# SwiGLU over 8192 rows: a first load in four interleaved transfers, an early gate on eight zeros, and five stores on GpSimd

## The chip, the cores and the metric

The kernel runs on one core of one Trainium2 chip. The metric is the device time of the whole program in microseconds (us), lower is better.

## The reference

```python
def reference(x):                      # x: 8192 x 8192, float32
    a, b = np.split(x, 2, axis=-1)     # two halves of 4096 columns
    silu_b = b / (1 + np.exp(-b))
    return a * silu_b                  # 8192 x 4096, float32
```

Every input element is read once (268.44 MB) and every output element written once (134.22 MB).

## The kernel before, in words

The 8192 rows are cut into 33 tiles in order of rows. Tile 0 and tile 32 have one row of x for each of the 128 partitions; the 31 tiles between have two. One row of x is 32 KB, so a full tile is loaded with 64 KB for each partition (8.39 MB) and stored with 32 KB for each (4.19 MB); tile 0 and tile 32 are half of that.

Three buffers in SBUF, `slot0` to `slot2`, take the tiles in turn: tile i lies in slot i modulo 3. For each tile there are four steps, and each belongs to one engine:

- `load` (line 51) is a DMA issued on SyncE (SP). Tile i+3 goes into the slot of tile i, so its load waits on SP until the store of tile i has landed.
- the gate (line 62) is SiLU on ScalarE (ACT), in place on the b half.
- the product (line 64) is a multiplication on VectorE (DVE), written over the front of the slot.
- `store` (line 77) is a DMA that waits for the product. It is issued from ACT's queue for tiles 0 to 29, and from SP's queue for tiles 30 to 32. Two of the earlier ones go to GpSimd (POOL) in place of ACT: the odd tiles from 16 to 19, that is 17 and 19.

The order of the instructions is the written one (`manual_schedule`): three loads first, then for each tile its gate, product, store, and the load three tiles ahead. Tiles 0 and 32 are gated and multiplied in two halves of 2048 columns, tiles 1 and 31 row by row. `follows_from_others` drops waits that are implied by others; `newest` remembers the last instruction on each engine for it. A DMA with 128 partitions is spread over the core's 16 DMA engines, with a packet for each contiguous row of a partition, and 16 small packets that signal its completion.

Of the kernel before, what the change touches and what calls it, by code (L numbers as in the profile page):

```python
# [1 line left out]

# [4 lines left out]

_SILU = mybir.ActivationFunctionType.Silu


@with_exitstack
def kernel(
    ctx: ExitStack,
    tc: tile.TileContext,
    x: bass.AP,
    out: bass.AP,
):

    nc = tc.nc  # L20
    N, M = x.shape
    half = M // 2
    P = nc.NUM_PARTITIONS
    BUFS = 3

    rows = [1] + [2] * (N // P // 2 - 1) + [1]
    first = [sum(rows[:i]) * P for i in range(len(rows))]
    last = len(rows) - 1

    pool = ctx.enter_context(tc.tile_pool(name="sbuf", bufs=1))  # L30
    ctx.enter_context(tc.manual_schedule())
    slots = [pool.tile([P, 2 * M], x.dtype, name=f"slot{s}") for s in range(BUFS)]
    loads, gates, prods, stores = ([[] for _ in rows] for _ in range(4))
    newest = {}

    def in_dram(t, i, width):

        return bass.AP(t.tensor, first[i] * width, [[rows[i] * width, P], [1, rows[i] * width]])

    def follows_from_others(inst, i, current, earlier):  # L40


        targets = [t for kind in current for t in kind[i]]
        targets += [t for kind in earlier for j in range(i % BUFS, i, BUFS) for t in kind[j]]
        for t in targets:
            if t is not newest.get(inst.ins.engine):
                tc.declare_no_dep(inst.ins, t.ins, reason="ordered by the other waits")
        newest[inst.ins.engine] = inst

    def load(i):  # L50
        inst = nc.sync.dma_start(  # L51
            out=slots[i % BUFS][:, : rows[i] * M], in_=in_dram(x, i, M)
        )
        follows_from_others(inst, i, [], [loads, gates, prods])
        loads[i].append(inst)

    def swiglu(i, k0, k1, c0=0, cw=half):
        view = slots[i % BUFS].rearrange("p (k s c) -> p k s c", k=2, s=2)
        a = view[:, k0:k1, 0, c0 : c0 + cw]
        b = view[:, k0:k1, 1, c0 : c0 + cw]  # L60
        o = slots[i % BUFS][:, : 2 * half].rearrange("p (k c) -> p k c", k=2)
        gate = nc.scalar.activation(out=b, in_=b, func=_SILU)  # L62
        follows_from_others(gate, i, [], [loads, gates, prods, stores])
        prod = nc.vector.tensor_mul(out=o[:, k0:k1, c0 : c0 + cw], in0=a, in1=b)  # L64
        follows_from_others(prod, i, [loads], [loads, gates, prods, stores])
        gates[i].append(gate)
        prods[i].append(prod)

    def by_halves(i):
        for c0 in range(0, half, half // 2):  # L70
            swiglu(i, 0, 1, c0, half // 2)

    def store(i):
        eng = nc.scalar if i < last - 2 else nc.sync
        if i % 2 and last // 2 <= i < last // 2 + 4:
            eng = nc.gpsimd
        inst = eng.dma_start(  # L77
            out=in_dram(out, i, half), in_=slots[i % BUFS][:, : rows[i] * half]
        )
        follows_from_others(inst, i, [loads, gates], [loads, gates, prods, stores])  # L80
        stores[i].append(inst)

    for i in range(BUFS):
        load(i)
    for i in range(last):
        if i == 0:
            by_halves(i)
        elif i in (1, last - 1):
            swiglu(i, 0, 1)
            swiglu(i, 1, 2)  # L90
        else:
            swiglu(i, 0, rows[i])
        store(i)
        if i + BUFS <= last:
            load(i + BUFS)
    by_halves(last)
    store(last)


# [1 line left out]
_INS = ['x']  # L101
_OUTS = [((8192, 4096), 'float32')]


# [23 lines left out]
```

## Time and profile before

| | us |
|---|---|
| median of three runs | 935.03 (934.96, 935.03, 940.76) |
| the profiled execution, its own time | 934.94 |
| span of its profile | 933.2 |
| DVE busy | 278.7 (30%) |
| ACT busy | 226.8 (24%) |
| POOL busy | 1.4 |
| moved by DMA | 402.67 MB, mean 432 GB/s |

The time of a run has 1.74 us beside the span of the profile. In the views, a line such as `L51 SPq DMA_DIRECT2D slot<-in_x_dram` is a DMA issue of line 51 on SP's queue; "to landing" is the time from the issue until the transfer's completion is signalled. The table of windows gives for each stretch of the span the busy time of the engines with the number of instructions, then the DMA share (1.00 is all 16 DMA engines busy) and GB/s. It counts a packet where it starts, so in very short windows it can be read as a count of packets: 32 KB in 0.25 us is 131 GB/s.

### The profile page before, as it was taken

Reading aid. Unit: us, or ns where it says so; the run is one execution under the profiler, and the core shown is the slowest. Engines: PE = TensorE matmul, PEld = TensorE weight load, DVE = VectorE, ACT = ScalarE, POOL = GpSimd, SP = SyncE. Lnnn points to the kernel's source line nnn. Section 1 sums busy time; section 2 is a strip of 40 time slices with the busy share of each in tenths; the row PEclk is TensorE's granted clock in tenths of the full one; section 3 lists DMA queues with packets and bytes.
Section 4 is the critical chain, followed back from the end, with each engine's and each line's share of the span. In section 5 each row is a group of like instructions: output and inputs, shape, how many; then the busy total and the mean of one; then the engine's idle time right before and its main releaser. Section 6 shows DMA issues by size and latency. Waiting matters only on the chain.

```text
span 933.2 us, 220 instructions
## 1 busy us (share of the span) xinstructions
DVE 278.7 (30%) x37; ACT 226.8 (24%) x38; POOL 1.4 (0%) x6
## 2 busy tenths in 40 slices
DVE  1312333123331233312333113332133321333242
ACT  2331133311333203332033320233202332023330
POOL 0000000000000000000000000000000000000000
DMA  9999999999999999999999999999999999999998
GB/s 405 405 449 431 423 451 444 409 444 433 444 427 434 442 410 448 428 433 442 434 421 441 445 417 444 428 454 427 420 457 405 449 427 428 448 445 409 427 444 388
DMA packets 9505, 402.67 MB, mean 432 GB/s; under 512 B 1056, under 2 KB 1056, under 8 KB 1056
## 3 DMA queue, kind: packets, MB, share of 16 engines
q1 hardware_dynamic: 5184, 278.92, 69.1%
q10 hardware_dynamic: 4032, 115.35, 28.6%
q0 software_dynamic: 288, 8.39, 2.1%
q14 instruction: 1, 0.01, 0.0%
HBM read 268.44 MB, written 134.22 MB: 431 GB/s over the span
## 4 chain that ended last, share of the span: by engine, by line
DMA 72%; DVE 11%; ACT 8%; issue 6%; another core or an unknown queue 1%; DVEq 0%; POOL 0%; SPq 0%; ACTq 0%; POOLq 0%
DMA slot<-in_x_dram 40%; DMA out_dram<-slot 32%; DVE slot L64 11%; ACT slot L62 8%; DVEq L123 0%; POOL out_dram L77 0%; SPq L51 0%; ACTq L77 0%; DVEq L64 0%; POOLq L123 0%
## 5 line engine op out<-in xcount | busy, mean ns | idle before, releaser
L64 DVE TENSOR_TENSOR slot<-slot 128x8192 f32<-128x8192 f32 (+2 forms) x37 | 278.7, 7539 | 636.7 <-ACT slot L62 636.5
L62 ACT ACTIVATE slot<-slot 128x8192 f32<-128x8192 f32 (+2 forms) x37 | 225.6, 6107 | 684.3 <-DMA slot<-in_x_dram 684.3
L77 POOL DMA_DIRECT2D out_dram<-slot x2 | 1.2, 600 | 568.9 <-DVE slot L64 568.9
L62 ACT ACT_TABLE_LOAD x1 | 1.3, 1283 | 0.7 <-PEq L112 0.7
L112 POOL MEMSET const-bfloat16-1.0<- 128x1 bf16 x1 | 0.1, 102 | 0.0
L112 POOL MEMSET const-float32-0.0<- 128x1 f32 x1 | 0.1, 99 | 0.2 <-issue 0.2
L112 POOL MEMSET const-float32-1.0<- 128x1 f32 x1 | 0.1, 99 | 0.0
L112 POOL MEMSET const-uint8-127<- 128x1 uint8 x1 | 0.1, 99 | 0.0
## 6 DMA issues: line engine op xcount, KB each, us to landing
out_dram<-slot ACTq DMA_DIRECT2D x27, 4096.0 KB, 33.5
slot<-in_x_dram SPq DMA_DIRECT2D x2, 4096.0 KB, 13.6
out_dram<-slot POOLq DMA_DIRECT2D x2, 4096.0 KB, 34.4
out_dram<-slot SPq DMA_DIRECT2D x2, 4096.0 KB, 20.4
out_dram<-slot ACTq DMA_DIRECT2D x1, 2048.0 KB, 28.1
out_dram<-slot SPq DMA_DIRECT2D x1, 2048.0 KB, 16.8
slot<-in_x_dram SPq DMA_DIRECT2D x31, 37.7
```

The costliest lines, as they stand in the source:

```text
L62: gate = nc.scalar.activation(out=b, in_=b, func=_SILU)
L64: prod = nc.vector.tensor_mul(out=o[:, k0:k1, c0 : c0 + cw], in0=a, in1=b)
L77: inst = eng.dma_start(out=in_dram(out, i, half), in_=slots[i % BUFS][:, : rows[i] * half])
L112: nc = _bacc.Bacc("TRN2", target_bir_lowering=False, num_devices=1)
```

## The change

The first load is no longer one transfer of 128 partitions but four, all on SP and one behind the other: partitions 0, 8, 16, ... (16 of them), then 4, 12, 20, ... (16), then 2, 6, 10, ... (32), then all the odd ones (64). Ahead of them, VectorE sets eight columns of `slot2` to zero and ScalarE runs SiLU on them; the load of tile 2, which writes the same slot, waits for that. And the odd tiles stored through GpSimd are those from 16 to 25: 17, 19, 21, 23 and 25, five in place of two.

```diff
+    def load_in_parts(i):
+
+        width = rows[i] * M
+        for p0, step in ((0, 8), (4, 8), (2, 4), (1, 2)):
+            inst = nc.sync.dma_start(
+                out=slots[i % BUFS][p0::step, :width],
+                in_=bass.AP(
+                    x.tensor, first[i] * M + p0 * width, [[step * width, P // step], [1, width]]
+                ),
+            )
+            newest[inst.ins.engine] = inst
+            loads[i].append(inst)
+
...
-        if i % 2 and last // 2 <= i < last // 2 + 4:
+        if i % 2 and last // 2 <= i < last // 2 + 10:
             eng = nc.gpsimd
...
-    for i in range(BUFS):
+
+    corner = slots[2][:, :8]
+    nc.vector.memset(corner, 0.0)
+    nc.scalar.activation(out=corner, in_=corner, func=_SILU)
+    load_in_parts(0)
+    for i in range(1, BUFS):
         load(i)
```

## The prediction

> **What bounds the kernel now.** I read the page first. No engine is busy for a third of the span, while the DMA row is full in every slice:
>
> ```profile
> DVE 278.7 (30%) x37; ACT 226.8 (24%) x38; POOL 1.4 (0%) x6
> DMA  9999999999999999999999999999999999999998
> q1 hardware_dynamic: 5184, 278.92, 69.1%
> q10 hardware_dynamic: 4032, 115.35, 28.6%
> q0 software_dynamic: 288, 8.39, 2.1%
> ```
>
> The shares of the three queues (SP's q1, ACT's q10, POOL's q0) add to 99.8% of what 16 DMA engines could do in the span. The chain that ended last names waits, but in a kernel whose transfers never pause they are a queue's length, not a cost. The windows say the same by stage; the columns are the stretch, its length, DVE, ACT and POOL busy, PE clock, DMA share, GB/s:
>
> ```profile
> 1.50:1.75 0.25, 0.00 (x0) 0.25 (x1) 0.00 (x0) 1.00 0.47 131
> 1.75:2.00 0.25, 0.00 (x0) 0.25 (x1) 0.00 (x0) 1.00 6.55 1704
> 2.00:2.25 0.25, 0.00 (x0) 0.01 (x1) 0.00 (x0) 1.00 0.45 131
> 2.25:2.50 0.25, 0.00 (x0) 0.00 (x0) 0.00 (x0) 1.00 0.40 131
> 2.50:3.50 1.00, 0.00 (x0) 0.00 (x0) 0.00 (x0) 1.00 0.00 0
> 3.50:3.75 0.25, 0.00 (x0) 0.00 (x0) 0.00 (x0) 1.00 1.21 524
> 3.75:4.00 0.25, 0.00 (x0) 0.00 (x0) 0.00 (x0) 1.00 2.42 1049
> 4.00:4.25 0.25, 0.00 (x0) 0.00 (x0) 0.00 (x0) 1.00 1.21 524
> ...
> 424.60:511.60 87.00, 26.09 (x4) 21.09 (x3) 0.00 (x0) 1.00 1.00 434
> 511.60:598.60 87.00, 26.08 (x4) 21.09 (x3) 1.20 (x2) 1.00 1.00 431
> 598.60:685.60 87.00, 25.92 (x3) 21.09 (x3) 0.00 (x0) 1.00 1.01 438
> ```
>
> Read as counts, 131 GB/s being one 32 KB packet, one DMA engine starts its first packet in 1.50 to 1.75, thirteen in the next quarter, one each in the two after: 16. The second packets start from 3.50 to 4.25 (4, 8, 4), so a first packet occupies its engine some 1.9 us. A later one takes 1.21 us (in 3.50 to 3.75 four packets fill a share of 1.21: 1.21 x 0.25 x 16 / 4), and 16 x 32768 B / 1.21 us is 433 GB/s, the rate of every later window. So the span is 1.9 us until the engines run, 0.7 us more for their first packet, then solid transfer to the end, and a last landing. Three things alone can move the time: the start, the rate, or a gap in the transfers. At 434 GB/s the 402.67 MB need 927.8 us, so no reordering can bring 1%, which is 9.35 us and about what a measurement of this kernel can tell from no change.
>
> **The change part by part.** *The split load.* It replaces one DMA issue by four on SP, with the same 128 packets of 32 KB and 48 more completion packets (three transfers of 16). SP's rows:
>
> ```profile
> 0.74 1.32 SPq L51 DMA_DIRECT2D slot<-in_x_dram  x3
> L51 SPq DMA_DIRECT2D slot<-in_x_dram x33: 327/328/425, 0.7 to 893.0; - x33
> DMA to landing us min/median/max: 12.2/37.7/59.2
> ```
>
> Three issues take 1.32 us from 0.74, so the fourth part is out by about 2.3, and tiles 1 and 2 are issued some 1.0 us (3 x 0.33) later, at about 2.5 and 2.8. Each DMA engine then has one packet from part 1 until about 3.75, one from part 2, two from part 3 and four from part 4: about eight packets to 12.5, before it needs tile 1. The delay of 1.0 us is covered by some 10 us of queued work; without that cover it would cost 1.0.
>
> What can be gained is the start. A transfer with one row per DMA engine has an eighth of the rows to prepare. The end is set by the last DMA engine, so at best its start moves from the 2.25 to 2.50 window to the 1.50 to 1.75 one (0.75 us), and the whole start cannot come before the issue itself has ended, at 1.1 (0.9 us from 2.0, where most have started). At worst nothing is gained. The nearest row is the spread itself: the stragglers start 0.25 to 0.5 us behind the thirteen. I take 0.3 us, and keep 0 and 0.9.
>
> What can be lost is the rate of the narrow parts; the trace has no transfer of fewer than 128 partitions. Lower bound 0: transfers that follow one another on SP leave no gap, for a window of 87 us with six transfers runs at 434, the packet rate itself. Upper bound: tile 0 took 12.2 us from issue to landing (the minimum above), its 4.19 MB at 433 GB/s are 9.7, so a transfer by itself has 2.5 us of fixed time; if each of three more parts paid that in full, 7.5 us. In between, if each new part paid a first packet's surplus, 0.7 us, it is 3 x 0.7 = 2.1. I take 0, since back-to-back transfers are the nearest row, and keep 7.5. The 48 completion packets cost nothing that a window shows: a boundary every 14.5 us leaves the rate at the packet rate.
>
> [...]
>
> *The early gate.* It adds one memset of 128x8 on DVE and one SiLU of 128x8 on ACT. The table load that stands before ACT's first gate is there already, and early:
>
> ```profile
> 0.73 1.28 ACT L62 ACT_TABLE_LOAD   x1 [0.73 <-PEq L112]
> 12.95 3.71 ACT L62 ACTIVATE slot<-slot 128x2048 f32<-128x2048 f32 x2 [10.94 <-DMA slot<-in_x_dram]
> ```
>
> It ends at 2.01, and ACT then idles 10.94 us. POOL's memsets of 128x1 take 0.1 us and a 2048-column gate 1.9, so the added pair costs between 0.1 and 2 us, nearer the former, inside that idle time: nothing, and nothing gained, since no table load stood on the path. But it adds a wait: tile 2's load stands on SP until the tiny gate is done, about 2.3 to 2.5, at most 4.0. Behind it on SP only tile 3's load is queued, which waits for the store of tile 0 until 47 anyway. Two tiles (12.6 MB, 29 us) are ahead of tile 2's packets. Cost 0; without that cover up to 1.2 us.
>
> *Three more stores on POOL* (21, 23, 25). They leave ACT's queue, where a store waits for DVE and holds the next gate; that gate waits for its load far longer (684.3 us in 33 waits), so nothing is gained. What POOL's queue costs is read from tiles 17 and 19:
>
> ```profile
> L77 POOL DMA_DIRECT2D out_dram<-slot x2: 533/600/667, 511.9 to 570.0; - x2
> out_dram<-slot ACTq DMA_DIRECT2D x27, 4096.0 KB, 33.5
> out_dram<-slot POOLq DMA_DIRECT2D x2, 4096.0 KB, 34.4
> ```
>
> The issue takes 0.60 us against 0.34, the landing comes 0.9 us later, and SP's load of tile i+3 waits for it. Three of these are 2.7 us of lateness, under a DMA that is full in those windows (431 and then 438 GB/s around the two, 434 in the mean). After them, the chain has stores of about 31.2 and loads of 40 us where it had 33.5 and 37.6: the shares shift, their sum stays at 71. On POOL's own queue nothing else stands. At the tail the shift matters most: tile 30's store is issued at 893.4 and lands 24.4 us later, at about 918, and tile 31's store is issued at about 911, so 7 us of overlap cover it. Two POOL stores moved the shares by 2.3 us; three more in proportion move 3.5, under 7. Cost 0; bounds from a gain of 0 (a full DMA gives none) to 2.7.
>
> [...]
>
> **Sum.** Against the profiled execution: 934.94 - 0.3 + 0 + 0 + 0 = 934.6 us (span 932.9 and the same 1.74 around it); 935.03, the median of the runs, lies 0.09 above that execution, so the two are the same.
>
> **The rivals.**
>
> *The parts do not start earlier* (the split does nothing of what it could): 934.9. For it: the first packet's 1.9 us is not the number of rows but a latency. Against: 16 starts spread over three quarters of a microsecond in the order of a preparation.
>
> *Each part pays a first packet's surplus:* 934.6 + 2.1 = 936.7. For it: first packets do take 0.7 us more. Against: back-to-back transfers show none.
>
> *The narrow parts run at a fraction of the rate*, on the other side, slower: if 16 or 32 partitions do not keep 16 DMA engines at 1.21 us a packet, nothing behind on the same queue can fill in, because tile 1 is behind them. Price 7.5 us, so 942.1; it decides as soon as the load of tile 0 lands later than now (12.95). Only at half rate for the whole load (9.7 us, 944.3) does it reach 1%.
>
> *The POOL stores open a gap:* 2.7 us, so 937.3, from the point at which the transfers still queued after a landing are less than 0.9 us of work. Against: the windows stay at 1.00 around the two that exist.
>
> **How the numbers follow.** Forecast 0.45; no earlier start 0.17; first-packet surplus 0.20; narrow parts slow 0.10; gap by POOL 0.08. The time is the forecast's, 934.6, with its own range 934.0 to 935.2 (the start's bounds and the distance of the runs shown). The low end of the whole range is the earliest start (0.9 us) with the same distance, 933.8. The high end takes in the surplus and the gap together, 934.6 + 2.1 + 2.7 = 939.4; only the slow parts, and a median among runs like 940.76, lie above. By cases, over 1% slower needs the half-rate load or more: 0.04. Over 1% faster has no mechanism: 0.01. Within 1%: 0.95.
>
> **What would show it.** In the profile after: first packets in a narrower band before 2.25; tile 0 landing at or before 12.95 (right) or after 14 (the narrow parts are slow, and 934.6 is wrong by what it is late); q0 at 720 packets with 431 to 438 GB/s in the windows of tiles 17 to 25; tile 2's issue before 4. A DMA share under 0.99 in any window between 20 and 890 would make the POOL part wrong.

## The result and the profile after

The changed kernel takes 936.95 us (median of 22 runs, 936.51 to 937.29) against 935.02 us of the kernel before (median of 22): 1.9 us more. The ratio is 1.0016, with a 95% interval of 1.001 to 1.0022. The move is small (0.2%), but it is resolved, and it goes the other way from the forecast of 934.6: it lies outside the forecast's own range (934.0 to 935.2) and inside the whole one (933.8 to 939.4). The ratios here and below are not quotients of the two medians; where an interval takes in 1.0, a difference of medians is unresolved.

The profiled execution took 936.83 us with a span of 934.8, so 1.6 of the 1.9 us lie inside the span; the other 0.3 is in what lies around it (2.03 against 1.74; over the 22 runs it was 1.73 to 2.19, with a median of 2.1). The three kernels below with one part of the change each have 1.72 to 1.84 there, so no single part shows this 0.3, and it stays open. From the page of the changed kernel, its engines, DMA row and queues:

```profile
DVE 278.7 (30%) x38; ACT 227.0 (24%) x39; POOL 3.0 (0%) x9
DMA  9999999999999999999999999999999999999999
q1 hardware_dynamic: 5232, 278.92, 69.2%
q10 hardware_dynamic: 3600, 102.76, 25.5%
q0 software_dynamic: 720, 20.97, 5.2%
```

The transfers still fill the span: 69.2 + 25.5 + 5.2 = 99.9%. SP's q1 has the 48 completion packets more (5184 to 5232), and q0 has gone from 288 to 720. The same windows at the start, of the changed kernel (DMA share and GB/s last; 524 GB/s in 1.00 us is 16 packets):

```profile
1.50:2.00 0.50, 0.00 (x0) 0.50 (x1) 0.00 (x0) 1.00 0.00 0
2.00:2.50 0.50, 0.00 (x0) 0.23 (x2) 0.00 (x0) 1.00 3.94 918
2.50:3.00 0.50, 0.00 (x0) 0.00 (x0) 0.00 (x0) 1.00 0.49 131
4.00:5.00 1.00, 0.00 (x0) 0.00 (x0) 0.00 (x0) 1.00 2.42 524
6.25:7.50 1.25, 0.00 (x0) 0.00 (x0) 0.00 (x0) 1.00 1.37 419
8.25:9.00 0.75, 0.00 (x0) 0.00 (x0) 0.00 (x0) 1.00 1.62 699
```

Each of the last three rows is one packet on each of the 16 DMA engines (GB/s times length is 524 KB), and the share times the length is what one packet took. The second packet, which is part 2 of the load (partitions 4, 12, ...), took 2.42 us; the third 1.37 x 1.25 = 1.71; from the fourth on 1.62 x 0.75 = 1.21, as every packet did before. And nothing starts before 2.0, where before fourteen engines had started by then. The second and third rows of packets in the kernel before:

```profile
3.50:4.25 0.75, 0.00 (x0) 0.00 (x0) 0.00 (x0) 1.00 1.61 699
4.75:5.50 0.75, 0.00 (x0) 0.00 (x0) 0.00 (x0) 1.00 1.62 699
```

Both are 1.21 us. The timeline of the changed kernel shows where the delay ends up (start, length, what):

```profile
0.74 2.52 SPq L61 DMA_DIRECT2D slot<-in_x_dram  x4
2.03 0.21 ACT L99 ACTIVATE slot<-slot 128x8 f32<-128x8 f32 x1
15.54 3.71 ACT L75 ACTIVATE slot<-slot 128x2048 f32<-128x2048 f32 x2 [13.30 <-DMA slot<-in_x_dram]
37.18 7.12 ACT L75 ACTIVATE slot<-slot 128x4096 f32<-128x4096 f32 x2 [17.93 <-DMA slot<-in_x_dram]
```

Tile 0's gate starts at 15.54 (12.95 before), 2.6 us late; tile 1's at 37.18 (35.47), 1.7 late; and the first gate of tile 31, near the end, at 900.03 (898.41), 1.6 late. So the loss is made in the first 15 us, 0.9 of it is won back by tile 1, and what is left is carried to the end nearly unchanged: with transfers that never pause, nothing behind tile 1 absorbed it.

### The profile page after: what moved, and what is told of

Read it like the earlier page. It is cut to its first block, busy times and chain, and to the rows that moved or that the text cites. A ratio compares the mean times of both kernels' runs of the same rounds, so it can differ in the third digit from the quotient of the medians.

```text
span 934.8 us, 232 instructions
## 1 busy us (share of the span) xinstructions
DVE 278.7 (30%) x38; ACT 227.0 (24%) x39; POOL 3.0 (0%) x9
## 3 DMA queue, kind: packets, MB, share of 16 engines
q1 hardware_dynamic: 5232, 278.92, 69.2%
q10 hardware_dynamic: 3600, 102.76, 25.5%
## 4 chain that ended last, share of the span: by engine, by line
DMA 72%; DVE 11%; ACT 8%; issue 6%; another core or an unknown queue 1%; SPq 0%; DVEq 0%; POOL 0%; ACTq 0%; POOLq 0%
DMA slot<-in_x_dram 39%; DMA out_dram<-slot 32%; DVE slot L77 11%; ACT slot L75 8%; SPq L61 0%; DVEq L141 0%; POOL out_dram L90 0%; ACTq L90 0%; DVEq L77 0%; POOLq L141 0%
```

## The experiments

Two theories stood against each other first. *The split:* its parts run slow by the partitions that they take, as part 2 did with 2.42 us a packet, and it carries the 1.9 us alone. *Stores, or a surplus for each transfer:* the loss comes from the POOL stores, the added wait, or a fixed price of each issue. All kernels are the one before with one edit.

**One part of the change at a time.**

```diff
# split_only
-    for i in range(BUFS):
+    load_in_parts(0)
+    for i in range(1, BUFS):
         load(i)
# gate_only
+    corner = slots[2][:, :8]
+    nc.vector.memset(corner, 0.0)
+    nc.scalar.activation(out=corner, in_=corner, func=_SILU)
# stores_only
-        if i % 2 and last // 2 <= i < last // 2 + 4:
+        if i % 2 and last // 2 <= i < last // 2 + 10:
```

> The kernel before with the split load alone (16, 16, 32, 64 partitions interleaved); no early gate, two stores on GpSimd. [...] Theory stores: the split is worth at most the later start, 0.4 us, and tile 0 lands late without the end moving.

> The kernel before with the early gate alone (eight zeros in slot2, SiLU on them, tile 2's load waits for it). Every theory but one: within 0.2 us of the kernel before. If the wait of tile 2's load on SP matters, 0.3 to 1.2 us slower.

> The kernel before with five stores on GpSimd in place of two, nothing else. [...] Theory stores: three more landings 0.9 us later each, or a slower transfer rate while they run, give 1 to 2.7 us more.

Measured, beside a kernel before at 935.09 (33 runs): the split alone 936.86 (ratio 1.0018, 1.0009 to 1.0026), the gate alone 935.16 (1.0, 0.9991 to 1.0009), the stores alone 935.38 (1.0, 0.9992 to 1.0009). The split carries the change; neither of the other two can be told from nothing (the stores are 0.3 us over by the medians). The windows of stores_only, from the first to past the last POOL store, agree:

```profile
511.00:598.00 87.00, 26.04 (x4) 21.09 (x3) 1.20 (x2) 1.00 1.00 435
598.00:685.00 87.00, 26.07 (x4) 21.09 (x3) 0.53 (x1) 1.00 1.00 434
685.00:772.00 87.00, 26.08 (x4) 21.09 (x3) 1.06 (x2) 1.00 1.00 434
```

The timeline of split_only also shows what the early gate is good for:

```profile
15.46 1.28 ACT L77 ACT_TABLE_LOAD   x1 [15.46 <-DMA slot<-in_x_dram]
```

With four transfers to wait for, the table load stands behind the wait, at 15.46 and no longer at 0.73 (with the two transfers of halves_interleaved below it is at 13.19); the early gate in the changed kernel puts it back to 0.73. It is worth 1.28 us on ACT, at a place where ACT has time: tile 0's gate starts at 16.75 there and at 15.54 in the changed kernel, tile 1's at 37.13 and 37.18. The medians of the two are 0.1 us apart; of the spans, split_only's is 0.2 longer (935.1 against 934.9), which the 0.3 around the changed kernel's span hides.

**The same split without the narrowest parts.** The first load goes in three interleaved transfers, of 32, 32 and 64 partitions.

```diff
-        for p0, step in ((0, 8), (4, 8), (2, 4), (1, 2)):
+        for p0, step in ((0, 4), (2, 4), (1, 2)):
```

> [...] Theory that any strided or narrow transfer pays a surplus of its own: 1.2 to 2 us, nearly as much as the split in four.

Measured: 935.62, ratio 1.0002 (0.9993 to 1.0011). Three strided transfers, one of them still of 32 partitions at the head, cost some 0.5 us by the medians, which the interval does not separate from none; the other 1.2 us of split_only belong to the two transfers of 16. At tile 0 the two kernels are further apart: its parts have all landed at 13.21 here and at 15.46 in split_only, where the stall at the end of this section is missing and makes up for some of it. The window of split_32_32_64 from 4 to 12 us:

```profile
4.00:12.00 8.00, 0.00 (x0) 0.00 (x0) 0.00 (x0) 1.00 1.03 442
```

These are 108 packets (442 x 8 us / 32.8 KB) of 1.03 x 8 x 16 / 108 = 1.22 us, so the two parts with a step of 4 ran at full rate. Why the third packets of the changed kernel, also with a step of 4, took 1.71 us no run settles; they start while other engines are still on part 2.

**Sets of partitions.** The next four split the first load in other ways; only the list of parts differs.

```diff
# eighths: 16 partitions each
+    parts = (0, 8), (4, 8), (1, 8), (5, 8), (2, 8), (6, 8), (3, 8), (7, 8)   # start, step
# halves_interleaved
+    parts = (0, 2), (1, 2)
# halves_contiguous
+    partitions 0:64, 64:128
# quarters_contiguous
+    partitions 0:32, 32:64, 64:96, 96:128
```

> The kernel before with the first load in eight transfers of 16 partitions (steps of 8, starting at 0, 4, 1, 5, 2, 6, 3, 7). [...] Theory fixed surplus per transfer (0.5 to 0.7 us each): 4 to 5.6 us. Theory later start alone: 0.4 us.

> The kernel before with the first load in two transfers, the even and the odd partitions. [...] Theory strides: a strided transfer of partitions is slower in itself, 1 us or more.

> The kernel before with the first load in two transfers, partitions 0 to 63 and 64 to 127, without a stride. [...] Theory strides or narrow transfers: 0 to 0.5 us more. It also shows whether the longer issue on SP (0.59 us where the whole load took 0.43) comes from the stride.

> The kernel before with the first load in four contiguous transfers of 32 partitions. [...] Theory fixed surplus per transfer: twice the cost of two halves.

| kernel (before: 935.26) | us | ratio, 95% interval |
|---|---|---|
| eighths | 943.97 | 1.0095 (1.008 to 1.011) |
| halves_interleaved | 935.55 | 1.0002 (0.9992 to 1.0012) |
| halves_contiguous | 944.74 | 1.0103 (1.0088 to 1.0118) |
| quarters_contiguous | 944.64 | 1.0101 (1.0086 to 1.0116) |

The two kernels with two transfers of 64 partitions differ by 9.2 us through nothing but which 64 partitions (and so which 64 rows of x) each transfer takes. A window of each, first halves_contiguous:

```profile
4.75:5.00 0.25, 0.00 (x0) 0.00 (x0) 0.00 (x0) 1.00 5.12 1049
slot<-in_x_dram SPq DMA_DIRECT2D x2, 2048.0 KB, 17.5
```

then halves_interleaved:

```profile
4.00:4.25 0.25, 0.00 (x0) 0.00 (x0) 0.00 (x0) 1.00 2.43 1049
slot<-in_x_dram SPq DMA_DIRECT2D x2, 2048.0 KB, 9.7
```

Both windows have eight packets (1049 / 131). They took 5.12 x 0.25 x 16 / 8 = 2.56 us each in the one and 1.21 in the other; the median time from issue to landing is 17.5 against 9.7. The eighths, from 4 to 12 us:

```profile
4.00:12.00 8.00, 0.00 (x0) 0.00 (x0) 0.00 (x0) 1.00 1.11 242
```

That is 59 packets of 2.4 us; the same window of quarters_contiguous (1.07, 221 GB/s) has 54 of 2.54. Two contiguous halves cost as much as four quarters (944.74 and 944.64 us), so it is not a price of each transfer; and it is not the stride, since the strided halves run at full rate (1.21 us a packet). Nor is it the longer issue on SP. The issue lines of halves_contiguous, halves_interleaved and quarters_contiguous, in this order:

```profile
L61 SPq DMA_DIRECT2D slot<-in_x_dram x2: 542/561/580, 0.7 to 1.3; - x2
L61 SPq DMA_DIRECT2D slot<-in_x_dram x2: 545/560/575, 0.7 to 1.3; - x2
L61 SPq DMA_DIRECT2D slot<-in_x_dram x4: 386/407/632, 0.7 to 2.1; - x4
```

The issues (shortest, median, longest in ns) are as long in the fast halves as in the slow ones, and shortest in the slow quarters. What makes them longer than the 0.33 us of a full load (0.37 for the first) is not settled. In the halves it is not the stride; for 32 partitions it may be, since the contiguous quarters take 0.41 us and the strided parts of split_32_32_64 0.54 to 0.59.

**Which side, HBM or SBUF.** A split of partitions is also a split of the HBM rows, so these runs leave a theory: the slow splits read rows at unlucky distances. Two kernels cross the sides; both leave the rows of tile 0 in another order in the output. "Ports" in their names stands for the partitions that are written; no run shows a port.

```diff
# hbm_halves_to_all_ports: HBM rows 0-63, 64-127 -> partitions 0::2, 1::2
# hbm_interleaved_to_half_ports: HBM rows 0::2, 1::2 -> partitions 0:64, 64:128
+            inst = nc.sync.dma_start(
+                out=slots[i % BUFS][p0 : p0 + step * (n - 1) + 1 : step, :width],
+                in_=bass.AP(
+                    x.tensor, first[i] * M + r0 * width, [[rstep * width, n], [1, width]]
+                ),
+            )
```

> The kernel before with the first load in two transfers that read the HBM rows of the two contiguous halves (as the slow contiguous halves did) but write them to the even and to the odd partitions; the rows of tile 0 so stand in another order in the output. [...] Theory HBM side (the slow splits are slow for the distance between the rows that are read at one time): 9 to 10 us over it.

> The mirror of it: the HBM rows are read interleaved, even then odd, as in the fast halves, and written to partitions 0 to 63 and 64 to 127; the rows of tile 0 so stand in another order in the output. [...] Theory HBM side: 0.2 to 0.6 us over it.

Measured, beside 935.02: 935.89 (1.0009, 1.0 to 1.0017) and 944.77 (1.0104, 1.0091 to 1.0117). The windows from 4 to 12 us, in the same order:

```profile
4.00:12.00 8.00, 0.00 (x0) 0.00 (x0) 0.00 (x0) 1.00 1.03 446
4.00:12.00 8.00, 0.00 (x0) 0.00 (x0) 0.00 (x0) 1.00 1.08 221
```

That is 1.21 us a packet in the one and 2.56 in the other. The time follows the partitions of SBUF that are written, not the rows of HBM that are read. The 0.9 us of the first is a little over the 0.3 of halves_interleaved, which writes the same partitions, at an interval that begins at 1.0.

**A stall in the kernel before that the change removes.** Tile 1 wins 0.9 us back. In the window 31.00 to 34.00, of the kernel before and then of the changed one:

```profile
31.00:34.00 3.00, 0.00 (x0) 0.00 (x0) 0.00 (x0) 1.00 1.00 350
```

```profile
31.00:34.00 3.00, 0.00 (x0) 0.00 (x0) 0.00 (x0) 1.00 1.01 437
```

350 GB/s in 3 us is 16 packets of 64 KB, one on each DMA engine, which fill the window (share 1.00): 3.0 us each, where the 64 KB packets of later windows take 2.42. The changed kernel has the full 437. This is 0.6 of the 0.9 us; another 0.15 are in the 16 packets that start from 21.5 to 23.0 in the kernel before (1.71 x 1.5 = 2.57 us each). It goes with the split in four: split_only has 437 GB/s in the window too, gate_only 350 and stores_only 360. The faster splits keep it: split_32_32_64 has 355 GB/s from 31.4 to 34.4 (share 1.01), halves_interleaved 350 from 31.5 to 34.5 (0.98). The eighths have 16 such packets of 2.9 us earlier, from 20 to 23 (0.97, 350). Two kernels tried whether it is how tile 0's store falls among the packets of tile 1.

```diff
# tile0_whole
-        if i == 0:
-            by_halves(i)
-        elif i in (1, last - 1):
+        if i in (1, last - 1):
# store0_pool
-        if i % 2 and last // 2 <= i < last // 2 + 4:
+        if i == 0 or i % 2 and last // 2 <= i < last // 2 + 4:
```

> The kernel before with tile 0 gated and multiplied in one piece of 4096 columns in place of two halves, so that its store is issued some 1.4 us later. In the profile of before, the last packet of tile 1's load on all 16 DMA engines takes 3.0 us in place of 2.4, from 31.1 on, and in the changed kernel it does not. Theory that this stall comes from how the store of tile 0 falls between the packets of tile 1: it moves or is gone, and 0.5 to 0.8 us are gained. Theory that it is set by something else: within 0.2 us of the kernel before.

> The kernel before with the store of tile 0 through GpSimd, that is on a third DMA queue and some 0.3 us later. The same two theories on the stall at 31.1 us: gone or moved with 0.5 to 0.8 us gained if it is how store and load packets meet; unchanged otherwise.

Neither gains: 936.52 (1.0021, 1.0011 to 1.0032; its runs lie from 935.08 to 940.22, and its profiled execution took 935.08) and 935.17 (1.0002, 0.9993 to 1.0011). That tile0_whole is 1.5 us slower by the median neither theory gave, and its profile, of its fastest run, can't show why. Both keep the stall: tile0_whole has 350 GB/s from 30.4 to 33.4 (share 1.01), store0_pool 360 from 31 to 34. So it is not set by when or on which queue tile 0's store goes out, as far as these two moved it. The cause of the stall stays open, and so does why its absence came with the slow start.

## Why the prediction was wrong, and where it was right

*The bound* was right: the transfers never pause, before or after (99.8% and 99.9% of what 16 engines could do in the span), so only the start, the rate or a gap could count. The change moved the time by 0.2% and not by 1%.

*The split's rate* is the step that failed. The prediction took 0, "since back-to-back transfers are the nearest row". But that row has transfers of 128 partitions, and a transfer to some of the partitions was exactly what was new; a row that lacks the disputed property says nothing on it. Measured: the part 2 packets cost 2.42 - 1.21 = 1.2 us, the third packets 1.71 - 1.21 = 0.5, and the first ones, which have 1.9 us of their own anyway, about 0.3 (3.94 x 0.5 x 16 / 14 = 2.25): 2.0 us where the sum had 0. With a start 0.4 later, that is most of the 2.6 us by which tile 0's gate is late; less the 0.9 of the stall it is the 1.6 at the end of the span. The runs show the rate by sets of partitions: steps of 2 (1.21 us a packet) and, at the head of split_32_32_64, of 4 (1.22) run at full rate; steps of 8 (2.4) and contiguous blocks of 32 (2.54) or 64 (2.56) at half of it. Why it is these sets no run shows, only that it is the partitions and not the rows that count.

*The start* was forecast 0.3 us earlier and came about 0.4 later. SP needed 0.62 us for the first narrow issue (0.74 to 1.35) where the whole load took 0.37, and its first packets begin after 2.0. The issues were sized at 0.33 and took 0.59, so the fourth part was out at 3.25 and not at about 2.3. In quarters_contiguous, whose first issue took 0.39, ten engines start between 1.75 and 2.0 again, so the late start goes with the long issue and not with the split as such. The first packets did not come in a narrower band either: they spread from 2.0 to 3.0. A transfer of one row for each engine had no earlier start, so the rival that the parts do not start earlier was right in that, and too mild.

*The rivals.* "The narrow parts run at a fraction of the rate" is what happened, given 0.10 and priced at 7.5 us. That the parts of 16 do not reach 1.21 us a packet was right; that it comes of being narrow was not, since strided parts of 32 reach it (1.22) and contiguous parts of 64 do not (2.56). The 7.5 us were three fixed times of 2.5, and what was paid was a slower rate in two packets of eight and part of a third. Where every part is narrow (eighths) or a contiguous block, the price is 8.7 to 9.5 us, which is near the half rate of the whole load (9.7) named there. The surplus of 2.1 gave 936.7, near the result, by a wrong reason: quarters cost what halves cost, so no surplus for each part shows.

*The test by tile 0's landing* caught it, but "wrong by what it is late" did not hold to the letter: 2.6 us late there, 1.6 at the end of the span, since the stall at 31 us went away. *The early gate* and *the POOL stores* cost nothing that can be told, as forecast. In the changed kernel the tiny gate is done at 2.24, and SP comes to tile 2's load only at 3.98, so that wait cost nothing; in gate_only the third load's issue ends at 2.59 in place of 2.06, also without harm. The POOL stores go through q0 with 720 packets, and the windows around them, from 513 to 774, have shares of 1.00, 1.00 and 0.99 at 435, 434 and 429 GB/s, so the last is a little under the 431 that was named.

## What to carry to other kernels

In these loads, which partitions a transfer takes set its rate, and not how many: interleaved halves (every second partition) and every fourth ran at full rate, 1.21 to 1.22 us for a packet of 32 KB; contiguous halves, quarters, or every eighth at half, 2.4 to 2.56 us. Here the transfers never pause, and 1.6 of the 2.6 us lost at the start were still there at the end; so a smaller first load helps only if it starts earlier at the full rate, and it did neither. When a step is priced by the nearest row, check that the row has the property in dispute; where no row has it, the other value belongs into the number's range as a case with a real chance (the slow parts had 0.10 here).

## What the runs showed of the hardware that was not expected

- Two interleaved halves of a load cost 0.3 us by the medians (unresolved), two contiguous ones 9.5: 2.56 us for a packet of 32 KB against 1.21, with the same bytes and queue; the crossed kernels show the same for either order of the rows.
- An issue on SP took 0.56 to 0.59 us in the median for these splits, contiguous halves included, and 0.41 for contiguous quarters, against 0.33 for a full load.
- With two or more transfers to wait for, ScalarE's table load went behind the wait of the first gate (from 0.73 us to 13.19 with two and 15.46 with four); in the changed kernel an early use of the function brings it back to 0.73.
- All 16 DMA engines spend 3.0 us on one 64 KB packet at 31 us in the kernel before, 0.6 more than on later ones. It is gone in the changed kernel and in split_only, and unexplained.
